# Merge gates of a hybrid decoder layer: the sigmoid moved from the input projection to the merge

## The chip, the cores and the metric

The kernel runs on one core of a Trainium2 chip. The metric is the device time of one execution in microseconds (us), lower being better; a single profiled execution supplies the trace. The engines are named as in the profile: PE does the matrix products (PEld its weight loads), DVE and POOL do elementwise work, ACT does activations, copies and casts and also issues some DMAs, and SP issues most DMAs.

## The reference, cut to what matters

One layer of a decoder trunk, with 512 tokens and width 2048, all in float32. One input projection makes everything the three branches need and the logits of the three merge gates. Each branch (a state-space scan, a causal mean pooling, a dilated attention) ends in a projection to the model width, and the merge weighs the three by the sigmoid of their gate logits:

```python
h = _rms_norm(x, norm_g[i])
proj = jnp.einsum("bld,dn->bln", h, w_in[i])
(z_ssd, xbc, dt, u_pool, z_pool, q, k, v, z_attn, gate_logits) = jnp.split(proj, IN_SPLITS, axis=-1)
...
gates = jax.nn.sigmoid(gate_logits.reshape(b, seq, N_BRANCHES, D_MODEL))
merged = (gates[:, :, 0] * (y_ssd @ w_br_ssd[i])
          + gates[:, :, 1] * (y_pool @ w_br_pool[i])
          + gates[:, :, 2] * (y_attn @ w_br_attn[i]))
x = x + merged @ w_out[i]
ple_gate = jax.nn.sigmoid(_rms_norm(x, ple_norm_g[i]) @ w_ple_gate[i])
x = x + ple_gate * (p[i] @ w_ple_proj[i])
```

## The kernel before, in words

**Products.** Every float32 product is made of three matmuls: each operand is split into a rounded part `hi` and a rest `lo`, and hi*hi, hi*lo and lo*hi are summed in PSUM. Weights are read from DRAM in entries of 512 KB. The list `plan` holds the entries in the order in which they are used, `load` (line 128) issues their DMAs on SP three entries ahead, and `split` makes `hi` with a copy on ACT (line 153) and `lo` with a subtraction on DVE (line 156). There are three buffers of each, and at the start of entry n the job calls `split(n + 2)`, so that the split runs two entries ahead of PE. A `hi` copy must wait until PE is done with the entry that had the buffer.

**Order.** The schedule is written by hand. `jobs` run one after the other; a job makes one group of output columns, entry by entry. After each entry `tick()` advances up to three generators (`other`, `tasks`, `third`) by one step, and with these the work of the branches is interleaved. Each engine executes its instructions in the order in which this code issues them. `job_a` makes four output tiles of 128 tokens by 512 columns, and calls `evac` for each after the last entry's matmuls have been issued. Its sums lie in PSUM banks of tag `g`; in the second half of the kernel there are five of them.

**The projection of q, k, v and the gates.** These columns are made by `s_block`, 1024 columns at a time, with seven products of half-size blocks in place of eight (a Strassen scheme). A block has three passes of four entries each, and its products are named L11, S2, S3, then S4, S1, then L12, L22. At the end of a pass `after` (lines 326 to 348) combines the sums: after S1 it forms the tiles of the right half with DVE adds (lines 340 and 341) and evacuates four of them, after L12 it evacuates two straight from PSUM into an `st` tile, and after L22 it subtracts on DVE (line 347) and evacuates two. So a block calls its evacuation eight times, six times with `src` and `o` the same tile and twice with a PSUM source. Five blocks make q, k, v and the gate of the attention output with `qkv_evac` (lines 571 to 577), then six blocks make the merge gates with `gate_evac` (lines 564 to 569), for the branches in the order 2, 0, 1. Both write their tile to DRAM with a DMA issued on ACT's queue: `qkv_d` and `gate_d`. After the last gate block the tile pools and the PSUM banks are assigned anew (line 631).

**The branches** follow, with pooling, attention and the scan interleaved; the last job before the merge ends in `z_evac` (lines 1174 to 1181), and `y_norm` (from line 1188 on) normalizes the scan's output: a matmul with ones (1192), a square root on ACT (1194), reciprocals on DVE (1196), the scaling of 16 tiles (1203) and their split (1211 and 1212).

**The merge** has 12 jobs: branch 2 (attention, 2 entries a job), then branch 0 (scan, 8 entries), then branch 1 (pooling, 8 entries), each for four groups `j` of 512 columns. Ahead of a job `load_gates` (line 1225) fetches its four gate tiles `g` from `gate_d` with DMAs on SP; one tile, of branch 1, `j` 0, `t` 3, is fetched at the end of `yp_stream`. The job's evacuation `ev` multiplies the gate by the sum in PSUM on DVE (line 1231), and from the second branch on POOL adds the product to `m` (line 1237). `y_norm` runs in the attention merge and into the scan's, `yp_stream` (splits of the pooled branch, line 400) from the last job of the scan's merge on, and `m_turn` (transposes and splits of the merged columns, lines 1274 to 1276) in the pooling's merge. The output projection and the second gate follow.

Of the kernel before, what the change touches and what calls it, by code (L numbers as in the profile page):

```python
# [11 lines left out]
AF = mybir.ActivationFunctionType  # L12
# [19 lines left out]
def hybrid_kernel(ctx: ExitStack, tc: tile.TileContext, x, p, norm_g, w_in, conv_w, conv_b, dt_bias, a_log,  # L32
# [3 lines left out]
    V, A, G, PE = nc.vector, nc.scalar, nc.gpsimd, nc.tensor  # L36
# [45 lines left out]
    def rows(t):  # L82
        return slice(t * 128, (t + 1) * 128)
# [86 lines left out]
    def job_a(w, c0, kn, xk, evac, pre=None, post=None):  # L170

        es = []
        for e in range(kn // 2):
            plan.append((w[e * 256:(e + 1) * 256, c0:c0 + L], 2, L))
            es.append(len(plan) - 1)

        def run():
            ps = {}
            for e, idx in enumerate(es):
                split(idx + (1 if idx < 4 else 2))  # L180
                hi, lo = parts.pop(idx)
                for t in range(4):
                    if e == 0:
                        ps[t] = PG()
                    for k in range(2):
                        kt = 2 * e + k
                        xh, xl = xk(kt, t)

                        product(ps[t], xh, xl, hi[:, k], lo[:, k], kt == 0, kt == kn - 1)
                if e == len(es) - 1:  # L190
                    for t in range(4):
                        evac(t, ps[t])
                    if post:
                        post()
                tick()
        jobs.append((pre, run))
# [366 lines left out]

    def gate_evac(br, j):
        def f(t, half, src, o):
            A.activation(o, src, AF.Sigmoid)  # L566
            c = (j + half) * L
            nc.scalar.dma_start(out=gate_d[br, rows(t), c:c + L], in_=o)  # L568
        return f
# [649 lines left out]
    def load_gates(br, j, ts=range(4)):  # L1219
        for t in ts:  # L1220
            if j == 3 and (t, 3) not in m and br != 2:
                m[t, 3] = T("m")
                nc.sync.dma_start(out=m[t, 3], in_=m_d[rows(t), :])
            gs[t, j] = T("g")
            nc.sync.dma_start(out=gs[t, j], in_=gate_d[br, rows(t), j * L:(j + 1) * L])

    def merge(br, w, kn, xk, first, last=None, after=None):
        def ev(j):
            def f(t, ps):
                g = gs.pop((t, j))  # L1230
                V.tensor_mul(g, g, ps)
                if first and j == 3:
                    G.dma_start(out=m_d[rows(t), :], in_=g)
                elif first:
                    m[t, j] = g
                else:
                    G.tensor_tensor(m[t, j], m[t, j], g, op=ALU.add)
            return f

        for j in range(4):  # L1240
            job_a(w, j * L, kn, lambda kt, t: tuple(a[:, rows(t)] for a in xk(kt)), ev(j),
                  pre=lambda j=j: (last() if last and j == 3 else None, load_gates(br, j, range(3 if (br, j) == (1, 0) else 4))),
                  post=(lambda j=j: after(j)) if after else None)
# [135 lines left out]
```

## Time and profile before

| | us |
|---|---|
| median of 3 runs | 2634.69 |
| the three runs | 2634.54, 2636.17, 2634.69 |
| the profiled execution, its own time | 2635.59 |
| its span, first to last instruction | 2633.9 |
| first and last start of the gates' Sigmoids (line 566) | 588.9 and 1009.9 |
| first and last start of the merge's products (line 1231) | 1873.0 and 2264.4 |

The times of the trace count from the start of the span. The mean granted clock of PE is 0.997 of full speed. In the lists of the trace a tile is written as `out<-in`; L566 is line 566 of the kernel; `x12` is a count; an entry in square brackets gives how long the engine had been idle before that instruction, and which instruction ended that. An engine's name with a q (ACTq, SPq) means its queue, where DMAs are issued. A matmul's end is modelled, its start is not.

### The profile page before, as it was taken

Reading aid. Unit: us, or ns where it says so; the run is one execution under the profiler, and the core shown is the slowest. Engines: PE = TensorE matmul, PEld = TensorE weight load, DVE = VectorE, ACT = ScalarE, POOL = GpSimd, SP = SyncE. Lnnn points to the kernel's source line nnn. Section 1 sums busy time; section 2 is a strip of 40 time slices with the busy share of each in tenths; the row PEclk is TensorE's granted clock in tenths of the full one; section 3 lists DMA queues with packets and bytes.
Section 4 is the critical chain, followed back from the end, with each engine's and each line's share of the span. In section 5 each row is a group of like instructions: output and inputs, shape, how many; then the busy total and the mean of one; then the engine's idle time right before and its main releaser. Section 6 shows DMA issues by size and latency. Waiting matters only on the chain.

```text
span 2633.9 us, 30270 instructions
## 1 busy us (share of the span) xinstructions
PE 2587.5 (98%) x11860; PEld 2127.8 (81%) x11860; DVE 1548.8 (59%) x1924; ACT 1007.4 (38%) x1277; POOL 191.3 (7%) x213
## 2 busy tenths in 40 slices
PE   7999999999999999999999999999999999999998
PEld 6778888887778787888888888877888888788887
DVE  5767777777777774554536567786642433233333
ACT  6434344444444443343434544543321322232322
POOL 2000000000000001101010001231011111000000
PEclk9999999999999999999999999999999999999999
DMA  6445555455554454434344444463443633333443
GB/s 220 119 140 176 177 165 159 147 160 167 169 175 144 146 158 144 120 104 144 113 143 123 128 123 140 124 187 110 154 148 113 210 108 125 104 121 112 130 142 96
DMA packets 237647, 374.52 MB, mean 142 GB/s; under 512 B 17208, under 2 KB 102020, under 8 KB 236992
## 3 DMA queue, kind: packets, MB, share of 16 engines
q1 hardware_dynamic: 218384, 331.31, 41.9%
q10 hardware_dynamic: 13904, 25.30, 2.6%
q0 software_dynamic: 5216, 15.98, 1.6%
q8 instruction: 93, 1.52, 0.2%
q14 instruction: 50, 0.41, 0.0%
HBM read 330.30 MB, written 42.23 MB: 141 GB/s over the span
## 4 chain that ended last, share of the span: by engine, by line
PE 89%; DVE 5%; ACT 3%; issue 1%; ACTq 1%; DMA 1%; POOL 0%; SPq 0%; DVEq 0%
PE pg L364 28%; PE pg L166 19%; PE pg L168 19%; PE pg L167 19%; ACT hi L153 1%; DVE lo L156 1%; ACT st L566 1%; PE ps L1079 1%; ACTq L568 1%; DVE bc L1032 0%; PE ps L797 0%; PE ps L761 0%; DMA x<-in_x_dram 0%; PE ps L1062 0%; PE ps L716 0%
## 5 line engine op out<-in xcount | busy, mean ns | idle before, releaser
L156 DVE TENSOR_TENSOR lo<-raw,hi 128x1024 fp32r<-128x1024 f32 x424 | 525.2, 1239 | 639.1 <-ACT hi L153 637.7
L153 ACT CAST hi<-raw 128x1024 fp32r<-128x1024 f32 x424 | 444.7, 1051 | 788.9 <-PE pg L168 435.1
L166 PE MATMUL pg<-hh,hi 128*128 128x512 f32 x1152 | 460.9, 400 | 2.3 <-ACT st L566 2.3
L168 PE MATMUL pg<-hh,lo 128*128 128x512 f32 x1152 | 449.8, 390 | 0.0
L167 PE MATMUL pg<-hl,hi 128*128 128x512 f32 x1152 | 449.4, 390 | 0.0
L166 PEld LDWEIGHTS pg<-hh,hi 128*128 128x128 f32 x1152 | 216.9, 188 | 50.3 <-issue 3.0
L168 PEld LDWEIGHTS pg<-hh,lo 128*128 128x128 f32 x1152 | 216.7, 188 | 45.9
L167 PEld LDWEIGHTS pg<-hl,hi 128*128 128x128 f32 x1152 | 217.0, 188 | 45.1 <-issue 2.4
L156 DVE TENSOR_TENSOR lo<-t,hi 128x1024 fp32r<-128x1024 f32 x132 | 161.6, 1225 | 102.2 <-ACT hi L153 101.8
L153 ACT CAST hi<-t 128x1024 fp32r<-128x1024 f32 x132 | 138.9, 1052 | 204.5 <-PE pg L364 165.2
L364 PE MATMUL pg<-lo,hh 128*128 128x512 f32 x528 | 207.1, 392 | 7.6 <-DVE lo L156 7.6
L364 PE MATMUL pg<-hi,hh 128*128 128x512 f32 x528 | 206.2, 391 | 1.6 <-ACT hi L153 1.6
L364 PE MATMUL pg<-hi,hl 128*128 128x512 f32 x528 | 205.5, 389 | 0.0
L364 PEld LDWEIGHTS pg<-lo,hh 128*128 128x128 f32 x528 | 99.1, 188 | 33.4 <-DVE lo L156 12.7
L364 PEld LDWEIGHTS pg<-hi,hh 128*128 128x128 f32 x528 | 99.1, 188 | 24.7 <-ACT hi L153 4.1
L364 PEld LDWEIGHTS pg<-hi,hl 128*128 128x128 f32 x528 | 99.1, 188 | 20.0
L166 PE MATMUL pg<-hi,mh 128*128 128x512 f32 x256 | 100.8, 394 | 0.0
L166 PE MATMUL pg<-hi,yph 128*128 128x512 f32 x256 | 100.1, 391 | 0.0
L167 PE MATMUL pg<-lo,mh 128*128 128x512 f32 x256 | 100.1, 391 | 0.0
L168 PE MATMUL pg<-hi,ml 128*128 128x512 f32 x256 | 100.0, 391 | 0.0
L166 PE MATMUL pg<-hi,xh 128*128 128x512 f32 x256 | 99.8, 390 | 0.0
L168 PE MATMUL pg<-hi,ypl 128*128 128x512 f32 x256 | 99.7, 389 | 0.0
(360 smaller groups left out, 4541.5 us busy)
## 6 DMA issues: line engine op xcount, KB each, us to landing
raw<-in_w_in_dram SPq DMA_DIRECT2D x320, 512.0 KB, 3.8
rs<-in_w_in_dram SPq DMA_DIRECT2D x44, 512.0 KB, 4.5
raw<-in_w_br_ssd_dram SPq DMA_DIRECT2D x32, 512.0 KB, 3.8
raw<-in_w_br_pool_dram SPq DMA_DIRECT2D x32, 512.0 KB, 3.8
raw<-in_w_out_dram SPq DMA_DIRECT2D x32, 512.0 KB, 3.7
raw<-in_w_ple_gate_dram SPq DMA_DIRECT2D x32, 512.0 KB, 3.7
gate_d<-st ACTq DMA_DIRECT2D x48, 256.0 KB, 2.2
g<-gate_d SPq DMA_DIRECT2D x48, 256.0 KB, 5.0
```

The source lines that it names most:

```text
L153: A.copy(hi, r)
L156: V.tensor_tensor(lo, r, hi.bitcast(F32), op=ALU.subtract)
L166: PE.matmul(ps, lhsT=lh, rhs=rh, start=first, stop=False)
L167: PE.matmul(ps, lhsT=lh, rhs=rl, start=False, stop=False)
L168: PE.matmul(ps, lhsT=ll, rhs=rh, start=False, stop=last)
L364: PE.matmul(ps[name][t], lhsT=lh, rhs=r[:, k], start=first and i == 0, stop=last and i == 2, skip_group_check=name in ("L11", "L12"))
L566: A.activation(o, src, AF.Sigmoid)
L568: nc.scalar.dma_start(out=gate_d[br, rows(t), c:c + L], in_=o)
L1079: PE.matmul(pd[q, rows(h // 2)], lhsT=xdt[:, h * 64:h * 64 + 64], rhs=bc[h // 4][:, rows(h % 4)], start=True, stop=True)
```

## The change

Two places change. `gate_evac` no longer takes the sigmoid: it copies the tile on ACT where it comes from PSUM, does nothing where source and target are the same tile, and writes the logits to `gate_d`. In the merge, ACT takes the sigmoid of the gate tile in place, just ahead of DVE's product.

```diff
     def gate_evac(br, j):
         def f(t, half, src, o):
-            A.activation(o, src, AF.Sigmoid)
+            if src is not o:
+                A.copy(o, src)
             c = (j + half) * L
             nc.scalar.dma_start(out=gate_d[br, rows(t), c:c + L], in_=o)
         return f
...
         def ev(j):
             def f(t, ps):
                 g = gs.pop((t, j))
+                A.activation(g, g, AF.Sigmoid)
                 V.tensor_mul(g, g, ps)
                 if first and j == 3:
                     G.dma_start(out=m_d[rows(t), :], in_=g)
```

## The prediction

> **What bounds the kernel now.** I read the page first, then the busy time by stretches, the waits of PE, and last the order of time of ACT, DVE and PE at a block's end.
>
> ```profile
> span 2633.9 us, 30270 instructions
> PE 2587.5 (98%) x11860; PEld 2127.8 (81%) x11860; DVE 1548.8 (59%) x1924; ACT 1007.4 (38%) x1277; POOL 191.3 (7%) x213
> ```
>
> PE is busy for 2587.5 of 2633.9 us. So a change that takes 36 operations off ACT in one stage and gives it 48 in another counts only where PE waits for ACT, or for DVE behind ACT. The projection holds a comparison made for this case: five blocks write q, k, v with `qkv_evac`, six write gates with `gate_evac`, and the same `s_block` code runs both. The first stretch below runs from the first `half=0` evacuation of the first qkv block to that of the fifth (four blocks), the second from the first gate block's to the sixth's (five blocks).
>
> ```profile
> 225.13:530.17 305.04, 305.04 (x1346) 252.02 (x1345) 237.37 (x225) 126.19 (x129) 0.00 (x0) 1.00 0.55 166
> 607.85:1003.21 395.36, 386.89 (x1681) 314.19 (x1680) 294.83 (x280) 175.59 (x190) 0.00 (x0) 1.00 0.52 157
> ```
>
> The columns are the stretch, its length, and the busy time of PE, weight load, DVE, ACT and POOL, then granted clock, DMA share and GB/s. A qkv block takes 305.04 / 4 = 76.26 us and PE is never idle in it. A gate block takes 395.36 / 5 = 79.07 us, and PE is idle for 395.36 - 386.89 = 8.47 us of the stretch. The clock is 1.00 in both, and the memory traffic is lower in the slower one. The waits of PE in the gate stage (us in total, times, longest):
>
> ```profile
> PE pg L364 <- DVE lo L156: 7.8, 12, 0.8
> PE pg L166 <- ACT st L566: 2.3, 1, 2.3
> PE pg L364 <- ACT hi L153: 1.6, 6, 0.5
> ```
>
> PE waits for the split of the weights (`hi` on ACT, `lo` on DVE). What delays the split is seen at a block's `S1` step, in the last gate block and in the second qkv block, each fence being one answer in order of time (start, duration).
>
> ```profile
> 983.55 0.68 DVE L340 TENSOR_TENSOR st<-st,pg 128x512 f32<-128x512 f32 x1
> ```
>
> ```profile
> 984.26 0.63 ACT L566 ACTIVATE st<-st 128x512 f32<-128x512 f32 x1 [1.89 <-DVE st L340]
> 984.92 0.33 ACTq L568 DMA_DIRECT2D gate_d<-st  x1
> ...
> 988.09 0.33 ACTq L568 DMA_DIRECT2D gate_d<-st  x1
> 988.51 1.05 ACT L153 CAST hi<-raw 128x1024 fp32r<-128x1024 f32 x1 [0.45 <-ACT st L566]
> ```
>
> ```profile
> 283.20 0.68 DVE L340 TENSOR_TENSOR st<-st,pg 128x512 f32<-128x512 f32 x1
> 283.91 2.12 ACTq L576 DMA_DIRECT2D qkv_d<-st  x4
> 286.15 1.05 ACT L153 CAST hi<-raw 128x1024 fp32r<-128x1024 f32 x1 [4.12 <-DVE st L341]
> ```
>
> From the first add to the next `hi`, the gate block takes 988.51 - 983.55 = 4.96 us and the qkv block 286.15 - 283.20 = 2.95 us. The 2.01 us between them come from four Sigmoids, each of which must end before its DMA is issued on the same queue, so that the DVE adds no longer set the pace.
>
> **Removed: the Sigmoids of the projection.** Per operation (duration min/median/max in ns):
>
> ```profile
> L566 ACT ACTIVATE st<-st x36: 629/632/634, 588.9 to 1009.9; 128x512 f32<-128x512 f32 x36
> L566 ACT ACTIVATE st<-pg x12: 598/598/598, 607.8 to 1004.6; 128x512 f32<-128x512 f32 x12
> L566 ACT ACT_TABLE_LOAD  x1: 1283/1283/1283, 587.0 to 587.0; - x1
> ```
>
> ```profile
> L574 ACT COPY st<-pg x10: 589/589/589, 225.1 to 531.5; 128x512 f32<-128x512 f32 x10
> ```
>
> 36 in-place ones go (36 x 0.632 = 22.8 us of ACT), 12 that move PSUM to `st` become copies (0.598 to 0.589 us each), and one table load goes (1.28 us). What matters is that `gate_evac` becomes `qkv_evac` but for the destination, DMA issues on ACT's queue included. So I price the stage as qkv blocks: 5 x (79.07 - 76.26) = 14.1 us. The first gate block's `S1` step lies between the two stretches:
>
> ```profile
> 530.11 0.59 ACT L574 COPY st<-pg 128x512 f32<-128x512 f32 x1 [0.26 <-PE pg L364]
> ```
>
> ```profile
> 607.85 0.60 ACT L566 ACTIVATE st<-pg 128x512 f32<-128x512 f32 x1 [0.26 <-PE pg L364]
> ```
>
> 607.85 - 530.11 = 77.74, against 76.26: 1.5 us more. Together 15.6 us. The waits view alone would give 7.8 + 1.6 = 9.4 us; I take the periods, since they are start times of like instructions, while an idle time depends on a modelled matmul end.
>
> **The end of the stage** has one more wait:
>
> ```profile
> 1008.13 1.28 DVE L347 TENSOR_TENSOR st<-st,pg 128x512 f32<-128x512 f32 x2
> 1008.85 0.63 ACT L566 ACTIVATE st<-st 128x512 f32<-128x512 f32 x1 [1.89 <-DVE st L347]
> 1009.56 0.47 PE L166 MATMUL pg<-hh,hi 128*128 128x512 f32 x1 [2.31 <-ACT st L566]
> ```
>
> PE's first matmul with newly assigned PSUM banks is put down to the Sigmoid, which ends at 1008.85 + 0.63 = 1009.48, but the last DVE reader of the old banks ends at 1008.13 + 1.28 = 1009.41, only 0.07 us sooner, and stays. I take 0; the ends are 0 and the whole 2.3 us. A loss has no source here, since every operation ahead of it stays or gets shorter.
>
> **Added: 48 Sigmoids in the merge.** They are 128x512 from SBUF to SBUF: 0.632 us each by the row above, 2.53 us for the four of a job, 30.3 us in all. In ACT's queue they stand after the `hi` copy made during a job's last entry, ahead of the scheduler's other steps and of the next `hi`. Each waits for its `g` load; behind it wait those `hi` copies and what `y_norm`, `yp_stream` and `m_turn` put on ACT, and DVE's product waits for it. They do not wait for PSUM, so they can run while PE is still in the entry. In the attention merge, where a job has only two entries:
>
> ```profile
> 1870.73 1.05 ACT L153 CAST hi<-raw 128x1024 fp32r<-128x1024 f32 x1 [2.51 <-PE pg L168]
> 1871.81 1.28 ACT L1194 ACT_TABLE_LOAD   x1
> 1877.76 0.63 ACT L1194 ACTIVATE zs<-v 128x512 f32<-128x512 f32 x1 [4.67 <-DVE v L1193]
> ...
> 1882.56 1.05 ACT L153 CAST hi<-raw 128x1024 fp32r<-128x1024 f32 x1 [3.24 <-issue]
> 1888.00 1.06 ACT L153 CAST hi<-raw 128x1024 fp32r<-128x1024 f32 x1 [4.39 <-PE pg L168]
> ...
> 1927.09 1.05 ACT L153 CAST hi<-raw 128x1024 fp32r<-128x1024 f32 x1 [3.35 <-PE pg L168]
> ```
>
> Job 0: a table load for Sigmoid, four Sigmoids, and the load for Sqrt again: 1871.8 + 1.28 + 2.53 + 1.28 = 1876.9, and Sqrt does not start before 1877.76, where DVE lets it go: hidden, with 0.9 us to spare. Job 1: from 1882.56 + 1.05 = 1883.6 one more table load and four Sigmoids end at 1887.4, ahead of the next `hi` at 1888.00 and of the job's products at 1889.29 (below). From there on no load is needed until Sqrt comes back in the output stage. In jobs 4 to 11, with eight entries, ACT stands idle 3.35 us before a `hi` even beside two `yh` copies, and 2.53 us fit in. A `hi` that is late costs nothing at once either: `split` runs two entries ahead, and an entry lasts 1888.00 - 1882.56 = 5.4 us.
>
> DVE's products, the issue of job 3's `g` loads, and the time from issue to landing of all 48 `g` loads:
>
> ```profile
> 1872.96 1.28 DVE L1231 TENSOR_TENSOR g<-g,pg 128x512 f32<-128x512 f32 x2
> 1877.03 0.69 DVE L1193 TENSOR_SCALAR v<-ps 128x512 f32<-128x512 f32 x1 [0.17 <-PE ps L1192]
> 1889.29 2.47 DVE L1231 TENSOR_TENSOR g<-g,pg 128x512 f32<-128x512 f32 x4
> ...
> 1907.77 1.28 DVE L1231 TENSOR_TENSOR g<-g,pg 128x512 f32<-128x512 f32 x2
> ```
>
> ```profile
> 1899.80 1.89 SPq L1225 DMA_DIRECT2D g<-gate_d  x4
> ```
>
> ```profile
> DMA to landing us min/median/max: 2.9/5.0/8.5
> ```
>
> Only job 0's first product starts later, at about 1873.7 for 1872.96; nobody waits for that, since the scheduler's next PSUM read stays at 1877.03 and the next job begins in the fifth of the five banks that jobs share. Job 3's loads, issued from 1899.80, land by about 1907 at the median, so its Sigmoids may end about 1908.5 and the yh copies behind them slip by a fraction of a us. Queues on SP and POOL keep their order; bytes are unchanged. I take 0 for the merge. Its bounds are 0 and, if all of it in the four short jobs were exposed, 4 x 2.53 + 2 x 1.28 = 12.7 us. A gain there is excluded, as nothing is removed.
>
> One price can be read two ways: what a table load costs.
>
> ```profile
> 1033.19 1.28 ACT L392 ACT_TABLE_LOAD   x1
> 1034.55 0.22 ACT L392 ACTIVATE small<-small 128x16 f32<-128x16 f32 x1
> ```
>
> The activation starts 0.08 us after the load's end, so 1.28 us is the whole price here. [...]
>
> **The sum.** 15.6 + 0 - 0 = 15.6 us. The profiled execution, 2635.59 us (span 2633.9), would become 2620.0. It lay 0.9 us above the median of 2634.69, so the median becomes **2619.1 us**. A measurement of this kernel can tell about 0.2%, 5.3 us, from no change.
>
> **Rivals.**
> 1. *Only the recorded waits come back*: 9.4 us, 2625.3. For it speaks the waits view; against it the whole periods, and a qkv block with the same matmuls. Chance 0.08.
> 2. *Dear table loads*: each holds ACT for as long again as it lasts (1.28 us more). Then job 0 needs 7.7 us where 6.0 are free, Sqrt is 1.7 us late, and with it the norm on which the next merge waits: 2620.8. The pair of rows above speaks against it. Chance 0.05. [...]
> 3. *Short jobs expose their Sigmoids*: late `g` loads hold ACT in the attention merge, 12.7 us are given back, 2631.8: no change. For it speaks a landing of up to 8.5 us; against it, that `split` is two entries ahead. Chance 0.05.
> 4. *The stall is not the Sigmoid's*, but comes of the gates' destination or place: 2634.7. The step from 2.95 to 4.96 us, Sigmoids alone, speaks against it. Chance 0.04.
> 5. *Slower*: ACT reaches the Sigmoids only when a job's sums are done, so that every product and the bank it frees come 2.53 us later in all 12 jobs: 30.3 + 2.6 - 15.6 = 17.3 us more, 2652.0. It decides from 1.3 us exposed per job. Against it: the copy in front of them starts with the job's last entry, 5.4 us before the sums end. Chance 0.03.
>
> **How the numbers follow.** The forecast itself has 0.75. Range 2616.5 to 2626.0: below, the 2.3 us of the stage's end; above, rivals 1 and 2 and about half of the short jobs' bound. Faster: forecast and rivals 1 and 2, 0.88; same: rivals 3 and 4, 0.09; slower: 0.03.
>
> **What would show it.** Right: PE idle near zero between the gate blocks' evacuations and a period near 76.3 us; about 2.9 us from the first `S1` add to the next `hi`; two more table loads in the attention merge, Sqrt not later against the products before it; PE's waits in the merge still about 3 us. Wrong: gate periods above 77 us, new waits of PE for `g` or `hi` after the SSD gate, or products held by ACT at the end of jobs.

## The result and the profile after

| kernel | median us (range, runs) | before beside it | ratio to before (95% interval) |
|---|---|---|---|
| changed | 2618.53 (2617.23 to 2619.11, 4) | 2635.43 | 0.9933 (0.9921 to 0.9944) |

The change makes the kernel 16.9 us faster by the medians; 15.6 were forecast. The profiled execution took 2617.23 us and happens to be the fastest of the four. Of its page, the lines that answer to those of before:

```profile
span 2615.5 us, 30296 instructions
PE 2579.6 (99%) x11860; PEld 2128.3 (81%) x11860; DVE 1548.5 (59%) x1924; ACT 1013.4 (39%) x1291; POOL 191.8 (7%) x213
```

DVE has the same work, ACT even 6 us more, and PE waits for them less. The two stretches of the projection, laid between the same evacuations as before (stretch, length, busy time of PE, PEld, DVE, ACT, POOL, then clock, DMA share, GB/s):

```profile
226.12:530.91 304.79, 304.79 (x1345) 252.08 (x1344) 237.27 (x225) 126.07 (x128) 0.00 (x0) 1.00 0.55 166
607.11:988.11 381.00, 381.00 (x1681) 315.10 (x1680) 295.06 (x280) 157.59 (x160) 0.00 (x0) 1.00 0.54 163
```

Five gate blocks take 381.00 us, 76.20 each, as a qkv block does (304.79 / 4), and PE is busy through all of it. The table shows where the rest of the two profiled executions differs; the limits are the `half=0` evacuation of the fifth qkv block, that of the sixth gate block, and the first `hi` of the attention merge behind which gates are used.

| stretch | before, us | after, us | difference |
|---|---|---|---|
| start to 530.11 / 530.91 | 530.11 | 530.91 | +0.8 |
| to 1003.21 / 988.11: six gate blocks | 473.10 | 457.20 | -15.9 |
| to 1870.73 / 1852.91: pooling, attention, scan | 867.52 | 864.80 | -2.7 |
| to the end of the span: merge, output, second gate | 763.17 | 762.59 | -0.6 |

The 15.9 us are the forecast. The 2.7 us are not, and a second profile of the same kernel (below) does not have them.

At the last gate block's `S1` step the four DMAs now follow the adds as in a qkv block. DVE, then ACT:

```profile
969.98 0.68 DVE L340 TENSOR_TENSOR st<-st,pg 128x512 f32<-128x512 f32 x1
```

```profile
970.70 2.12 ACTq L569 DMA_DIRECT2D gate_d<-st  x4
972.93 1.06 ACT L153 CAST hi<-raw 128x1024 fp32r<-128x1024 f32 x1 [4.13 <-DVE st L341]
```

From the first add to the next `hi` it is 972.93 - 969.98 = 2.95 us where it was 4.96. At the end of the stage PE waits almost as long as before, and is now put down to the operation that was given as the true one:

```profile
992.74 1.28 DVE L347 TENSOR_TENSOR st<-st,pg 128x512 f32<-128x512 f32 x2
...
994.16 0.47 PE L166 MATMUL pg<-hh,hi 128*128 128x512 f32 x1 [2.01 <-DVE st L347]
```

In the merge, ACT's order of time in the four short jobs:

```profile
1853.98 1.28 ACT L1232 ACT_TABLE_LOAD   x1
1855.28 2.19 ACT L1232 ACTIVATE g<-g 128x512 f32<-128x512 f32 x4
1857.49 1.28 ACT L1195 ACT_TABLE_LOAD   x1
1859.93 0.63 ACT L1195 ACTIVATE zs<-v 128x512 f32<-128x512 f32 x1 [1.16 <-DVE v L1194]
...
1865.81 1.28 ACT L1232 ACT_TABLE_LOAD   x1
1867.11 2.20 ACT L1232 ACTIVATE g<-g 128x512 f32<-128x512 f32 x4
1870.18 1.06 ACT L153 CAST hi<-raw 128x1024 fp32r<-128x1024 f32 x1 [0.88 <-ACT g L1232]
...
1880.36 0.64 ACT L1232 ACTIVATE g<-g 128x512 f32<-128x512 f32 x1 [1.08 <-DMA g<-gate_d]
```

The square root still waits for DVE, 1.16 us after ACT is ready. Job 1's Sigmoids end 0.88 us before the next `hi`. Only one of the 48 had to wait for its load. The waits of PE in the merge, before (from 1860 us to 2275) and after (from 1840 to 2256):

```profile
PE ps L1274 <- POOL m L1237: 1.8, 2, 0.9
PE pg L166 <- DVE g L1231: 0.7, 1, 0.7
PE ps L1274 <- DVE ml L1276: 0.5, 1, 0.5
```

```profile
PE ps L1276 <- POOL m L1239: 1.8, 2, 0.9
PE pg L166 <- DVE g L1233: 0.7, 1, 0.7
```

48 Sigmoids have added no wait.

### The profile page after: what moved, and what is told of

It reads as the page before. It is cut to its first block, busy times and chain, and to the rows that moved or that the text cites. A ratio compares the mean times of both kernels' runs of the same rounds, so it can differ in the third digit from the quotient of the medians.

```text
span 2615.5 us, 30296 instructions
## 1 busy us (share of the span) xinstructions
PE 2579.6 (99%) x11860; PEld 2128.3 (81%) x11860; DVE 1548.5 (59%) x1924; ACT 1013.4 (39%) x1291; POOL 191.8 (7%) x213
## 4 chain that ended last, share of the span: by engine, by line
PE 94%; DVE 3%; ACT 2%; issue 1%; DMA 1%; SPq 0%; POOL 0%; ACTq 0%; DVEq 0%
PE pg L364 32%; PE pg L166 19%; PE pg L167 19%; PE pg L168 19%; PE ps L1080 1%; PE ps L798 0%; DMA x<-in_x_dram 0%; PE ps L762 0%; PE ps L1063 0%; ACT hi L153 0%; PE ps L717 0%; PE ps L1069 0%; PE ps L1276 0%; DVE lo L156 0%; DVE bc L1033 0%
## 5 line engine op out<-in xcount | busy, mean ns | idle before, releaser
L364 PEld LDWEIGHTS pg<-hi,hh 128*128 128x128 f32 x528 | 99.1, 188 | 20.8
```

What stands on the lines that cost most here:

```text
L364: PE.matmul(ps[name][t], lhsT=lh, rhs=r[:, k], start=first and i == 0, stop=last and i == 2, skip_group_check=name in ("L11", "L12"))
```

## Experiments

The theory: a Sigmoid that stands between a DVE add and the DMA of its tile, on the queue that also makes the `hi` copies, delays the split, and in the merge the same Sigmoids are hidden. The rivals: the merge costs something that the sum hides; it is ACT's work as such, the function or its table; or the place and the target of the gate blocks. Times in us; kernels with one value of "before" ran together.

| kernel | median (range, runs) | before | ratio (95% interval) | gate block, us |
|---|---|---|---|---|
| removal alone | 2619.54 (2618.18 to 2621.22, 5) | 2636.01 | 0.9939 (0.9926 to 0.9951) | 76.20 |
| addition alone | 2635.78 (2632.78 to 2638.57, 11) | 2636.01 | 1.0000 (0.9991 to 1.0008) | 79.04 |
| only the tiles behind S1 | 2626.34 (2624.15 to 2628.04, 5) | 2636.01 | 0.9961 (0.9948 to 0.9975) | 77.37 |
| Sigmoid kept, DMA issued by POOL | 2621.91 (2619.85 to 2623.38, 5) | 2636.01 | 0.9947 (0.9935 to 0.9960) | 76.16 |
| changed, once more | 2619.92 (2616.92 to 2622.76, 4) | 2635.59 | 0.9941 (0.9926 to 0.9956) | 76.19 |
| a copy in the Sigmoid's place | 2634.45 (2632.24 to 2635.84, 10) | 2635.59 | 0.9995 (0.9986 to 1.0005) | 78.83 |
| Sigmoid in the qkv blocks | 2631.65 (2630.20 to 2635.01, 10) | 2635.59 | 0.9988 (0.9979 to 0.9997) | 76.19 |
| merge, three times the work | 2629.71 (2627.69 to 2631.95, 10) | 2635.59 | 0.9978 (0.9969 to 0.9988) | 76.19 |
| the same, eight-entry jobs only | 2622.35 (2620.81 to 2624.98, 4) | 2635.69 | 0.9950 (0.9934 to 0.9967) | 76.19 |
| the same, first short job only | 2626.29 (2624.78 to 2628.28, 5) | 2635.69 | 0.9965 (0.9952 to 0.9978) | 76.18 |

### Removal alone

```diff
                 g = gs.pop((t, j))
-                A.activation(g, g, AF.Sigmoid)
                 V.tensor_mul(g, g, ps)
```

> The gate evacuation is that of the changed kernel, and the merge multiplies by the bare logits: the Sigmoid is left out of the computation altogether, so that this is the removal alone. My theory (the whole gain lies in the projection and the 48 Sigmoids of the merge are hidden): the same time as the changed kernel, 2618.5 us within 2, with the gate blocks at 76.2 us. Rival, the merge costs something that the measured sum hides: faster than the changed kernel by what it costs, 2606 to 2615 us (up to 12.7 us from the four short jobs).

2619.54 us, 16.5 below before: no faster than the changed kernel (16.9 below, and 15.7 in its second set of runs). Leaving the 48 Sigmoids out gains nothing that these runs, with intervals some 3 us to each side, can tell.

### Addition alone

```diff
(in the kernel before)
                 g = gs.pop((t, j))
+                A.activation(g, g, AF.Sigmoid)
                 V.tensor_mul(g, g, ps)
```

> The kernel before with the merge's Sigmoid added, so that gates go through it twice (another value of the gates): the addition alone. My theory: as the kernel before, 2635 us within 2, gate blocks at 79.1 us, PE's waits in the merge still about 3 us. Rival, Sigmoids exposed in the short jobs: up to 12.7 us more, 2648; exposed in all jobs: 2668.

The ratio is 1.0000, its interval 0.9991 to 1.0008, which excludes a cost above 2.1 us. With the run before, the first rival is out.

### Only the tiles behind S1

```diff
-            if src is not o:
-                A.copy(o, src)
+            if half == 0:
+                A.activation(o, src, AF.Sigmoid)
...
-                A.activation(g, g, AF.Sigmoid)
+                if j % 2:
+                    A.activation(g, g, AF.Sigmoid)
```

> Half of the change: the four tiles that follow S1 are stored without their sigmoid, which the merge takes in column groups 1 and 3; the tiles after L12 and L22 keep it in the projection. My theory (each Sigmoid between a DVE add and the DMA issued for its tile delays the split behind it, at S1 by about 1.5 us a block, at L22 by about 1.3 us): 6 x 1.5 = 9 us of the 17 come, 2626 us (2624 to 2628), with a block period of 77.6 us. Rival, the gain goes with ACT's work removed (24 of 48 Sigmoids, 24 in place of 36 in-place ones): by 24/36 of the gain, 2623.5 us. Rival, all of it is the S1 step: 2619 us.

2626.34 us: 9.7 below before, near the 9 us that the price of 1.5 us (S1) a block gives. The rival of S1 alone (2619) is out. The rival by ACT's share of work (2623.5) is not: the interval reaches from 2622.3 to 2629.4 us. The block period does not decide between the two either. It is 77.37 us, for 77.6 by the theory and 77.16 by the rival (79.07 less 24/36 of 2.87). The next run is the one that tells them apart.

### Sigmoid kept, DMA issued by POOL

```diff
(in the kernel before)
             A.activation(o, src, AF.Sigmoid)
             c = (j + half) * L
-            nc.scalar.dma_start(out=gate_d[br, rows(t), c:c + L], in_=o)
+            G.dma_start(out=gate_d[br, rows(t), c:c + L], in_=o)
```

> The kernel before, Sigmoids in place, but the gates' DMAs issued on POOL's queue instead of ACT's. My theory (what delays the split is the alternation in one queue: each Sigmoid must end before its DMA is issued, 1.04 us a tile, while the DVE adds take 0.6 us a tile): the four Sigmoids follow the adds without a gap, the next hi copy starts 1.5 to 2 us sooner after S1, and most of the gain comes, 2619 to 2624 us. Rival, the Sigmoid's own work on ACT (0.63 us a tile) is what delays the split: 2632 to 2636 us.

This run decides what the stall is made of. The Sigmoids are all there, and five blocks take as little time as without them, with PE busy throughout. The stretch of the gate blocks, and ACT at the last block's `S1`:

```profile
607.60:988.40 380.80, 380.80 (x1681) 315.45 (x1680) 295.02 (x280) 174.29 (x190) 21.58 (x40) 1.00 0.52 163
```

```profile
970.99 2.42 ACT L566 ACTIVATE st<-st 128x512 f32<-128x512 f32 x4 [1.89 <-DVE st L340]
973.32 1.03 ACT L153 CAST hi<-raw 128x1024 fp32r<-128x1024 f32 x1
```

Four Sigmoids take 2.42 us in one piece instead of 4 x 1.04 us in alternation with four DMAs. ACT is busy 174.29 us, nearly as before (175.59), so the Sigmoids' own work does not make the stall. It takes the Sigmoid (0.63 us) and the issue (0.33 us) of each tile one after the other in one queue: 1.04 us a tile with the gaps between them, where the DVE adds come every 0.6 us. With either of the two gone from the queue, ACT keeps up with the adds: four Sigmoids alone take 2.42 us, four issues alone 2.12 us in the changed kernel. That the order alone would do it, with the four issues behind the four Sigmoids on ACT's queue, is not shown; no such run was made. An issue takes 0.33 us, against a median of 2.2 us from issue to landing for these DMAs in the kernel before. The small time counted all the same: four issues, with the gaps beside them, stood ahead of the `hi` copy on which PE's next products depend, and without them the kernel took 14.1 us less of 2636.0.

By the medians the kernel is still 2.4 us slower than with the Sigmoids removed. Its profile has a longer end: the last output DMA is issued at 2612.75 us and the span ends at 2621.3, 8.6 us later, against 2629.20 and 2633.9, 4.7 us, in the kernel before. What holds the end of the program there stays open.

### A copy in the Sigmoid's place

```diff
-            if src is not o:
-                A.copy(o, src)
+            A.copy(o, src)
```

> The changed kernel, but the gate evacuation copies each tile on ACT, also in place where source and target are the same tile: an ACT operation of the Sigmoid's length that computes nothing. My theory (it is an ACT operation between the DVE add and the DMA issue on one queue that delays the split, whatever it computes): the gain is gone, 2634 to 2637 us, gate blocks at 79 us. Rival, the function or its table matters: 2619 us.

2634.45 us, ratio 0.9995 with 1 inside the interval: the gain is gone although nothing is computed. ACT at the last block's `S1`:

```profile
983.90 0.62 ACT L566 COPY st<-st 128x512 f32<-128x512 f32 x1 [1.89 <-DVE st L340]
984.55 0.33 ACTq L568 DMA_DIRECT2D gate_d<-st  x1
...
987.67 0.33 ACTq L568 DMA_DIRECT2D gate_d<-st  x1
988.09 1.05 ACT L153 CAST hi<-raw 128x1024 fp32r<-128x1024 f32 x1 [0.45 <-ACT st L566]
```

It is the same alternation, and neither the function nor its table makes the stall.

### Sigmoid in the qkv blocks

```diff
(in qkv_evac)
-            if src is not o:
-                A.copy(o, src)
+            A.activation(o, src, AF.Sigmoid)
```

> The changed kernel with a Sigmoid put into the evacuation of q, k, v and the attention's gate (their values are changed by it), to turn the comparison of the two kinds of blocks round. My theory: the qkv blocks now take 79.1 us, the gate blocks 76.2 us, 5 x 2.8 = 14 us more than the changed kernel, 2632 to 2634 us. Rival, the place or the target of the gate blocks made the difference: 2619 us.

The first four qkv periods and the five gate periods of this run:

```profile
227.73:543.41 315.68, 309.37 (x1345) 251.37 (x1344) 236.85 (x225) 140.49 (x152) 0.00 (x0) 1.00 0.50 160
620.70:1001.63 380.93, 380.93 (x1681) 315.07 (x1680) 295.10 (x280) 157.66 (x160) 0.00 (x0) 1.00 0.52 163
```

The stall has moved to the other blocks, 315.68 / 4 = 78.92 us each, and the gate blocks are free of it. So place and target have no part in it. In all it is 11.7 to 13.1 us slower than the changed kernel's two medians, for 14 expected.

### Changed, once more

> The changed kernel once more, for a second profile. My theory: the projection's gain of 16 us stays, and what the first profile showed beyond it, 2.4 us in the scan's stage and 0.6 us at the end of the merge, depends on how waits of PE fall against its granted clock and may be there or not: 2617 to 2620 us. Rival, those 3 us belong to the change: they are there again at the same places.

2619.92 us. This profiled execution took 2622.76 us, 5.5 more than the first, with the gate blocks the same to 0.1 us. By the starts of like matmuls, 2.5 us of the difference arise in the scan's stage, 1.6 at the change of banks after the gate blocks, and 0.7 each ahead of the gate blocks and at the end of the merge. In the scan's stage 1.1 us are a wait of PE for `bc` (line 1055), which the kernel before has too and the first profile of the changed kernel has not; 1.5 us come with PE's granted clock, which was half for 6.83 us there, as in the kernel before, and for 3.41 us in the first profile (see the last section). The 2.7 us of the first profile are thus not tied to the change.

### Merge, three times the work

```diff
                 A.activation(g, g, AF.Sigmoid)
+                for _ in range(2):
+                    A.copy(g, g)
                 V.tensor_mul(g, g, ps)
```

> The changed kernel with two more copies in place behind each Sigmoid of the merge, so that ACT has three times the work added, 6.6 us a job. My theory (the split runs two entries ahead, an entry lasts 5.4 us, and ACT is idle 3 to 4 us in each): the jobs with eight entries hide it, the four short ones may lose up to 1 us each: 2618 to 2623 us. Rival, the cover is no larger than the 2.2 us a job that the change uses: 12 x 4.4 = 53 us more, 2672 us.

2629.71 us: about 10 us lost, more than I expected, and far less than the rival's 53. Against the first profile of the changed kernel, and by the starts of like matmuls, PE loses 6.9 us in the first two short jobs, nothing from there to the last products, and 3.7 us behind these. The 12 us of the expectations below are not PE's time: `hi` copies of the short jobs come up to 11.8 us later, counted from what they were late ahead of the merge, but they stand on ACT behind the added copies, and PE is not held up by all of that. Two more runs took this apart.

### The same in the eight-entry jobs only, and in the first short job only

```diff
-                for _ in range(2):
+                for _ in range(2 if not first else 0):              # eight-entry jobs
+                for _ in range(2 if first and j == 0 else 0):       # first short job
```

> The changed kernel with the two extra copies behind each Sigmoid only in the eight jobs with eight entries. My theory now: those jobs hide three times the work, and only the very last one, behind whose products the transposes wait, loses the 3.7 us that the run with copies in all jobs showed there: 2622 to 2625 us. Rival, the long jobs cost something each: 8 x 1 us and more, 2628 us or above.

> The changed kernel with the two extra copies only in the first job of the attention merge, ahead of the square root of the scan's norm. My theory now: the change leaves some 1.2 us of room ahead of that square root, the copies need about 5 us, so that it and the norm behind it come some 4 us late: 2622 to 2625 us. Rival, the delay grows along the norm and alone makes the 12 us that the short jobs lost: 2630 to 2633 us. Rival, the norm has room further on: 2619 us.

With the eight long jobs loaded, 2622.35 us: 2.4 to 3.8 us above the changed kernel. In the profile the long jobs lose nothing up to the last products, and 3.7 us there. With the first short job alone loaded, 2626.29 us: 6.4 to 7.8 us above, for the theory's 4 and the first rival's 12. Its profile shows why the price is more than the square root's delay. ACT, then PE, then two stretches (columns as above, the clock third from the end):

```profile
1867.27 1.28 ACT L1195 ACT_TABLE_LOAD   x1
1868.61 0.63 ACT L1195 ACTIVATE zs<-v 128x512 f32<-128x512 f32 x1
```

```profile
1876.49 0.50 PE L167 MATMUL pg<-lo,yah 128*128 128x512 f32 x1 [1.64 <-DVE lo L156]
1880.88 0.79 PE L166 MATMUL pg<-hi,yah 128*128 128x512 f32 x1 [2.94 <-DVE g L1235]
```

```profile
1875.10:1878.51 3.41, 1.45 (x5) 0.86 (x5) 3.41 (x6) 0.61 (x1) 0.00 (x0) 1.00 0.23 76
1878.51:1885.34 6.83, 4.46 (x11) 3.50 (x12) 6.83 (x11) 0.00 (x0) 0.00 (x0) 0.50 0.58 180
```

Against the first profile of the changed kernel the root starts 8.7 us later, and 4.5 us of that had arisen before the merge: it is 4.2 us late, as the theory said. Then PE waits 1.64 + 2.94 us, where the changed kernel waits 0.7 us, and the clock is half for 6.83 us. The eleven matmul starts from 1880.88 on take 4.69 us, which would be 2.5 us at 0.227 us each, so that the clock costs 2.2 us by this estimate. Together these make 6.1 us, and behind the job PE's matmuls start 6.2 us later. So the delay does grow along the norm, and the first short job makes nearly the whole loss of the short jobs, as the first rival had it; but that loss is 6.9 us and not 12.

## Why the prediction was right

**The projection.** Pricing the gate blocks as qkv blocks was right: 76.20 us a block for 76.26, 15.9 us in the profile for 15.6. Rival 1, the recorded waits alone (9.4 us), is out. In the stage before, matmuls start 0.227 us apart where nothing holds them and are drawn 0.39 us long, so a late start shows 0.16 us less of idle time than it costs. In the five blocks 35 starts are late, by 14.05 us together, where the idle time is 8.47 us; the period from one like instruction to the next misses nothing. That an ACT operation in the Sigmoid's place makes the difference is shown by the copy there and by the Sigmoids in the other blocks, and that it takes the DMA's issue on the same queue besides is shown by the DMAs issued elsewhere. Rival 4 is out by the same runs.

**The end of the stage.** The value of 0 was right: 2.31 us of wait became 2.01, behind the last DVE reader of the old banks, as argued from the 0.07 us between the two ends.

**The merge.** The value of 0 was right, by the trace and by the removal and the addition alone; rivals 3 and 5 are out. The room ahead of the square root is 1.16 us, where 0.9 were worked out, as four Sigmoids in a row take 2.19 us instead of 4 x 0.632. Job 2, not job 3, had a Sigmoid that waited for its load, 1.08 us, at no cost.

**The table loads.** Their number went as said: one less in the projection, two in the attention merge, and one more when the square root comes back in the output stage.

```profile
L392 ACT ACT_TABLE_LOAD x7 | 9.0, 1283 | 0.1
L1232 ACT ACT_TABLE_LOAD x2 | 2.6, 1283 | 0.0
```

At line 392 there were six before. Rival 2 is out: 1853.98 + 1.28 = 1855.26, and the first Sigmoid starts at 1855.28; the 1.28 us more that the rival gave a load is its assumption and shows in no run. The load itself starts 0.02 us behind the `hi` copy ahead of it, which ends at 1852.91 + 1.05 = 1853.96. The Sigmoids in front of the square root, with the two loads more, cost nothing here, because ACT has time to spare behind them, 1.16 us in job 0 and 0.88 us in job 1. The room is small: about 5 us more of ACT work in the first short job cost 6 to 8 us.

**What the sum did not have.** The median moved by 16.9 us in one set of runs and by 15.7 in the other; 15.6 lies in both intervals (14.8 to 20.8 and 11.6 to 19.5 us). The profiled execution's further 2.7 us in the stage of pooling, attention and scan differ from one execution of a kernel to the next: 1.1 us are the wait for `bc`, and 1.3 us come with a half clock that lasted 6.83 us before and 3.41 us after.

## What to carry to other kernels

An engine that is 38% busy can still hold up the kernel by what stands in its queue ahead of the work that PE needs: here the DMA of a tile was issued 0.03 us after the end of the Sigmoid that made it, the issue took 0.33 us more, and everything behind it on the queue came later. Look for two groups of like work in one trace that differ in one operation, and compare their periods rather than the waits. Work put on an idle engine was free here up to the first thing that waited for it: some 1.2 us ahead of the square root, and in each long job the 5 us or so of eight copies, which cost no time up to the last products.

## What was not expected of the hardware

Behind some of PE's waits its granted clock was half, for 3.41 us or for 6.83 us, so that the loss went on when the wait was over. Two such stretches start at 1783.78 and 2268.47 us in the kernel before, 484.69 us apart, which is 142 times 3.4133; two start at 1767.98 and 2249.26 us in the first profile of the changed kernel, 481.28 us apart, 141 times 3.4133. Below are periods of 3.41 us, counted from such starts, and the stretches that follow them. First the scan's wait of 4.33 us in the kernel before, and the stretch behind the same wait in the changed kernel:

```profile
1780.37:1783.78 3.41, 0.10 (x1) 0.00 (x0) 2.75 (x4) 3.38 (x5) 0.00 (x0) 1.00 0.87 281
1783.78:1790.61 6.83, 5.80 (x25) 4.70 (x26) 6.69 (x12) 0.76 (x1) 2.95 (x2) 0.50 0.46 130
```

```profile
1767.98:1771.39 3.41, 3.11 (x19) 2.59 (x20) 3.31 (x5) 0.03 (x1) 2.66 (x2) 0.50 0.52 162
```

Then the end of the merge before, where PE waited 0.9 us twice and then 0.5 us:

```profile
2265.06:2268.47 3.41, 1.53 (x10) 1.10 (x10) 0.59 (x2) 1.14 (x3) 1.85 (x2) 1.00 0.77 252
2268.47:2271.88 3.41, 3.19 (x10) 2.71 (x11) 2.53 (x5) 1.95 (x3) 0.00 (x0) 0.50 0.00 0
```

Last the change of banks, before and in the second profile of the changed kernel, with a wait of 2.3 and of 2.0 us:

```profile
1005.55:1008.96 3.41, 1.71 (x8) 1.09 (x6) 1.97 (x3) 1.17 (x2) 0.00 (x0) 1.00 0.84 227
1008.96:1012.37 3.41, 2.81 (x12) 2.36 (x13) 0.45 (x1) 2.20 (x3) 0.00 (x0) 1.00 0.89 282
```

```profile
992.80:996.21 3.41, 1.40 (x7) 1.14 (x7) 1.93 (x3) 1.02 (x1) 0.00 (x0) 1.00 0.77 210
996.21:999.62 3.41, 3.41 (x10) 2.67 (x9) 0.00 (x0) 0.03 (x1) 0.00 (x0) 0.50 0.70 253
```

In the period just ahead of a half clock PE was busy for 0.10 and 1.53 us in the kernel before, for 0.00 us (from 1764.57) and 1.56 us (from 2245.85) in the first profile of the changed kernel, for 1.40 us in the second, and for 1.45 us in the run with the first short job loaded. The periods from 1005.55, with 1.71 us, and from 5.42, with 1.24 us, both in the kernel before, were followed by full clock. What sets off the half clock was thus not shown. The two waits at the change of banks are nearly equal, and behind only one of them was the clock half. Behind the merge PE is busy but slow, as its order of time shows:

```profile
2270.89 0.63 PE L166 MATMUL pg<-hi,mh 128*128 128x512 f32 x1
2271.31 0.63 PE L167 MATMUL pg<-lo,mh 128*128 128x512 f32 x1
2271.74 0.47 PE L168 MATMUL pg<-hi,ml 128*128 128x512 f32 x1
2272.04 0.40 PE L166 MATMUL pg<-hi,mh 128*128 128x512 f32 x1
2272.28 0.39 PE L167 MATMUL pg<-lo,mh 128*128 128x512 f32 x1
2272.51 0.39 PE L168 MATMUL pg<-hi,ml 128*128 128x512 f32 x1
```

The matmuls start 0.43 us apart until 2271.74, and 0.23 to 0.24 us apart from 2272.04 on; the half clock lasted until 2271.88.

The half clock makes part of the differences between executions of one kernel, 1.5 and 1.6 of the 5.5 us between the two profiles of the changed kernel. Where all of the rest comes from was not shown.
